# Gated-parallel decoder step: both transposes of a softmax block in one step, its values one step sooner

## The chip, the cores and the metric

One program on one core of one Trainium2 chip. The metric is device microseconds of one execution. The core has five engines with instruction queues of their own that run side by side and wait for each other through semaphores: TensorE (PE, with its weight loads listed as PEld), VectorE (DVE), ScalarE (ACT), GpSimd (POOL) and SyncE (SP), which here only issues transfers between the memory of the device and that of the core. Each engine works through its queue in order, so an instruction that waits holds up all that stand behind it on its engine.

## The reference

One decoder layer on 1024 prompt tokens and 64 sample tokens (8 sequences of 8), in float32:

```
u = rmsnorm(x); [a | q | k | v | g_a | g_b] = u @ w_in
branch A: multi-scale pooling of a, a linear map for each group, @ w_pa
branch B: 3 head groups of 4 heads, (window, dilation) = (128,1), (512,4), (2048,16):
    qb = query blocks of 128;  kb, vb = the block itself and the block before it
    s = qb . kb * 64**-0.5, masked;  p = exp(s - max) ;  den = sum(p);  o = p . vb / den
    the 3 groups' outputs are combined by weights proportional to their denominators, @ w_pb
h = x + (sigmoid(g_a) * A + sigmoid(g_b) * B) @ w_o
y = h + relu(rmsnorm(h) @ w_up)**2 @ w_down
```

The change touches the prompt's part of branch B alone: `p . vb` needs `p` with keys on the partitions, so the softmax is transposed before it is multiplied with the values.

## The kernel before, in words

Float32 matrices are split into two rounded parts, and each product of weights is made of three passes over these parts, so nearly all of the time is matmuls of 128x128 weights. The program runs in stages: the pooling input, then the queries, keys and values of group 2 (dilation 16), group 1 (dilation 4) and group 0 (dilation 1), then the gates, the two output branches, `w_o`, and the two halves of the feed-forward layer.

The attention is woven into the three middle stages. `qkv_part` makes one projection of one block of 128 tokens (`pqk` queries and keys together, `pq`, `pk` or `pv` one of them, each some 3 to 6 us of matmuls), and then calls `step()`; the wide ones (`pqk`) also call it in their middle. `step()` runs every pending piece of side work forward to its next `yield`: each is a Python generator, and what it issues between two yields stands on PE's queue between two pieces of projection. The order on PE is exactly the order in which the kernel issues (`manual_schedule`); on the other engines a scheduler sets it when the kernel is built, by its own estimate of times, so a move on PE also moves rows on DVE, ACT and the transfer queue.

For each block `b` of each group there is one generator: `attend` transposes the block's queries and keys (`tq`, line 673), and `attend_rest` goes on to `attention`, the function that changes. Its parts, by the lines of the profile:

- scores `sg` (line 690): matmuls of 64 rows, two heads side by side, into two PSUM tiles, one for each value of `e`
- softmax: for each of four heads a masked minimum on DVE (line 699, tile `sm`) and an exponential on ACT (line 700); the heads of `e` = 0 come first
- two yields, and then for each `e` the transposes `tp` (line 709) on PE, the copy of them to `pT` on ACT (line 712), and a yield
- values `po` (line 723): matmuls that fill 64 columns of the array, from both `pT`, and a copy to the tile `oc` on ACT (line 730, 733 or 736)

A block of group 0 after the first has two blocks of keys (`nk` = 2), as has every second block of group 1; the others have one, and half the transposes, scores and values. After `attention`, `attend_rest` stores `oc` (line 824) or, in group 0, starts `combine` (transposes `tw` of the weights, line 782, and spreading matmuls `sw`, line 791), and the store of its result (line 797). All transfers between the memories that the passage names go through SP's queue.

The buffers rotate: `short` gives PSUM tiles from four, `sm` and `pT` have two each.

Names: in the tables `tpg2b0` or `pog1b6` are the transposes of group 2, block 0 and the values of group 1, block 6; the profile leaves block numbers out (`tpg2b`). `L116` on ACT and `L117` on DVE split weights that have come in (`raw_qkv`), `L657` scales queries or keys by their norm, `L664` copies a block's values out of PSUM, `L602` copies a block's tokens into natural order (`natt`), `L511` belongs to the pooling.

Of the kernel before, what the change touches and what calls it, by code (L numbers as in the profile page):

```python
# [37 lines left out]
def decoder_step(ctx, tc, i, o):  # L38
# [10 lines left out]
    def rr(p, shape, dt, name, tag, bufs):  # L49

        n = turn[p, tag] = turn.get((p, tag), -1) + 1
        return p.tile(shape, dt, name=name, tag=f"{tag}.{n % bufs}", bufs=1)
# [183 lines left out]
    def short(name):  # L236

        spare[0] = (spare[0] + 1) % 4
        if spare[0] == 4:
            return acc_p.tile([P, 512], F32, name=name, tag="acc.3", bufs=1)  # L240
        return ps.tile([P, 512], F32, name=name, tag=f"t.{spare[0]}", bufs=1)

    def short4(name):
        return short(name).rearrange("p (a b) -> p a b", a=4)
# [346 lines left out]
    def res8(blk):  # L591
        return blk // 2 + 4 * (blk % 2)
# [85 lines left out]
    def attention(g, b, keys, qT, name):  # L678


        st = md[:, b, 0, :] if g == 0 else sta[g][:, res8(b), :]
        nk = len(keys)
        mask = m3 if g == 2 else (m1 if nk == 2 else m1[:, P:])
        W = nk * P
        sc = [short(f"s{name}_{e}").rearrange("p (a b) -> p a b", a=2) for e in range(2)]
        for hp in range(2):
            for j, (kT, _) in enumerate(keys):
                for e in range(2):
                    rows = slice(e * HD, (e + 1) * HD)
                    t_.matmul(sc[e][:, hp, j * P:(j + 1) * P], qT[rows, hp, :], kT[rows, 2 + hp, :], start=True, stop=True)  # L690
        done.add(name)
        sms = []
        for e in range(2):
            sm = rr(ap, [P, 2, 256], F32, name=f"sm{name}_{e}", tag="sm", bufs=2)
            sms.append(sm)
            for hp in range(2):
                h = 2 * hp + e

                v_.tensor_tensor_reduce(sm[:, hp, :W], sc[e][:, hp, :W], mask, -1.0, -NEG, ALU.add, ALU.min, st[:, h:h + 1])
                s_.activation(sm[:, hp, :W], sm[:, hp, :W], AF.Exp, bias=st[:, h:h + 1], scale=-1.0,  # L700
                              accum_out=st[:, 4 + h:5 + h])
        yield
        yield
        pTs = []
        for e in range(2):
            tp = short4(f"tp{name}_{e}")
            for hp in range(2):
                for j in range(nk):
                    t_.transpose(tp[:, hp * nk + j, :], sms[e][:, hp, j * P:(j + 1) * P], ident)  # L709
            pT = rr(ap, [P, 4, P], F32, name=f"pT{name}_{e}", tag="pT", bufs=2)  # L710
            pTs.append(pT)
            s_.copy(pT[:, :2 * nk, :], tp[:, :2 * nk, :])
            if g == 0 and b % 2 and e == 0:
                assert {(1, "max"), (2, "max")} <= done
                of_pair[b // 2] = weights(b // 2)
            yield
        po = short(f"po{name}")[:, :256].rearrange("p (j t) -> p j t", j=2)

        for hp in range(2):
            for j, (_, vr) in enumerate(keys):  # L720
                for e in range(2):
                    h = 2 * hp + e
                    t_.matmul(po[e * HD:(e + 1) * HD, hp, :], vr[:, h * HD:(h + 1) * HD], pTs[e][:, hp * nk + j, :],  # L723
                              start=(j == 0), stop=(j == nk - 1))
        if b % 2 == 0:
            assert g or b < 4 or ("c", b // 2 - 2) in done
            pair[g] = rr(ap, [P, 512], F32, name=f"oc{name}", tag="oc", bufs=2)
        if g == 2:
            dst = pair[g].rearrange("p (u j l s) -> p j u l s", u=4, j=2, s=2)
            s_.copy(dst[:, :, :, :, b % 2], po.rearrange("p j (u l) -> p j u l", u=4))  # L730
        elif g == 1:
            dst = pair[g].rearrange("p (u j l) -> p j u l", u=4, j=2)
            s_.copy(dst[:, :, b % 2 * 2:b % 2 * 2 + 2], po.rearrange("p j (u l) -> p j u l", u=2))
        else:
            dst = pair[g].rearrange("p (j q l) -> p j q l", j=2, q=4)
            s_.copy(dst[:, :, :, b % 2 * 32:(b % 2 + 1) * 32], po.rearrange("p j (l q) -> p j q l", q=4))
# [4 lines left out]
    def weights(u):  # L741


        nm, den = md[:, 2 * u:2 * u + 2, :, :4], md[:, 2 * u:2 * u + 2, :, 4:]
        mm = ap2.tile([P, 2, 4], F32, name=f"cm{u}", tag="cm2")
        e = ap2.tile([P, 2, 3, 4], F32, name=f"ce{u}", tag="ce2")
        w = ap2.tile([P, 2, 3, 4], F32, name=f"cw{u}", tag="cw2")
        hl = ap2.tile([P, 2, 2, 3, 4], F32R, name=f"hl{u}", tag="hl")
        over = lambda t: t.unsqueeze(2).to_broadcast([P, 2, 3, 4])
        behind_pe(v_.tensor_reduce(mm, nm.rearrange("p b g h -> p b h g"), axis=AX.X, op=ALU.min))  # L750
        v_.tensor_tensor(e, over(mm), nm, op=ALU.subtract)
        s_.activation(e, e, AF.Exp)
        v_.tensor_tensor(w, e, den, op=ALU.mult)
        v_.tensor_reduce(mm, w.rearrange("p b g h -> p b h g"), axis=AX.X, op=ALU.add)
        v_.reciprocal(mm, mm)
        v_.tensor_tensor(w, e, over(mm), op=ALU.mult)
        s_.copy(hl[:, :, 0], w)
        v_.tensor_tensor(hl[:, :, 1], w, hl[:, :, 0].bitcast(F32), op=ALU.subtract)
        return hl.rearrange("p b s g h -> p b (s g h)").bitcast(F32)
# [1478 lines left out]
```

## Time and profile before

| | |
|---|---|
| time, 3 runs | 1402.63 us median (1401.01 to 1406.38) |
| the profiled execution | 1407.21 us, of which the span of its records is 1405.4 us |
| busy in the span | PE 1394.7 us (99%), PEld 1344.4, DVE 958.3, ACT 753.7, POOL 255.3 |
| mean granted TensorE clock | 0.999 of full speed |
| attention woven into the projections | about 90 to 416 us of the span |

PE is busy for 99% of the span. Its busy time is a modelled one: a matmul is listed with its whole passage through the array, and matmuls that follow each other overlap, so a short wait or a change of shape is hidden in the busy time. The start times don't hide it: what a group of matmuls costs the queue is the time from its start to the start of the next group. In the rows of the timeline the first column is the start in us from the span's beginning, the second how long the group took, and a bracket at the end gives idle time of the engine before it and what ended it.

### The profile page before, as it was taken

The page shows a single profiled execution, that of the slowest core. Times are in us where ns is not written, and L with a number is a line of the kernel's source. Part 1 is how long each engine was busy: PE and PEld are TensorE (multiplying, and loading weights), DVE is VectorE, ACT ScalarE, POOL GpSimd, SP SyncE. Part 2 cuts the span into 40 slices and gives each one's busy share as a digit, 9 for nine tenths or more (in the row PEclk, how much of TensorE's full clock was granted, in tenths as well). Part 3 has the DMA queues.
Part 4 walks back from the last instruction along what each step waited for, and adds up shares of the span by engine and source line. Part 5 has one row for each costly group of instructions (what it writes and reads, how often), then busy time and mean ns, then how long its engine had stood idle before and what let it go on. Part 6 is the DMA issues. An engine that isn't in the chain of part 4 may idle for free.

```text
span 1405.4 us, 29330 instructions
## 1 busy us (share of the span) xinstructions
PE 1394.7 (99%) x11101; PEld 1344.4 (96%) x11101; DVE 958.3 (68%) x1714; ACT 753.7 (54%) x1778; POOL 255.3 (18%) x362
## 2 busy tenths in 40 slices
PE   9999999999999999999999999999999999999998
PEld 8988987887999999999999999999999999999998
DVE  7778744776776767876468678665665686664566
ACT  8556775787765323563336455454554544444443
POOL 0744355676500000000000000000000000000100
PEclk9999999999999999999999999999999999999999
DMA  6455876755477777975468668856758988787674
GB/s 215 132 178 169 252 234 211 223 137 141 123 255 228 247 233 239 314 237 176 133 200 285 227 221 275 267 195 213 251 191 270 332 275 261 230 245 231 206 257 169
DMA packets 180701, 311.96 MB, mean 222 GB/s; under 512 B 26824, under 2 KB 82574, under 8 KB 178511
## 3 DMA queue, kind: packets, MB, share of 16 engines
q1 hardware_dynamic: 174926, 258.04, 57.0%
q0 software_dynamic: 5632, 52.04, 11.5%
q8 instruction: 87, 1.43, 0.4%
q14 instruction: 56, 0.45, 0.1%
HBM read 239.94 MB, written 122.12 MB: 258 GB/s over the span
## 4 chain that ended last, share of the span: by engine, by line
PE 70%; DMA 2%; DVE 1%; ACT 0%; issue 0%; SPq 0%; DVEq 0%; ACTq 0%
PE pz L1318 23%; PE pd L2096 23%; PE pg L1318 11%; PE ph L200 7%; PE pab L1318 4%; DMA raw_ab<-in_w_ab_dram 1%; DMA raw_d<-in_w_down_dram 0%; ACT places L116 0%; PE pog0b L723 0%; PE sg0b L690 0%; PE tpg0b L709 0%; PE pk L200 0%; PE pv L200 0%; SPq L127 0%; DVE places L117 0%
## 5 line engine op out<-in xcount | busy, mean ns | idle before, releaser
L2096 PE MATMUL pd<-places 128*128 128x272 f32 x2688 | 332.0, 287 | 0.7 <-DVE t L1960 0.7
L2096 PEld LDWEIGHTS pd<-places 128*128 128x128 f32 x2688 | 331.6, 188 | 0.9 <-DVE t L1960 0.9
L116 ACT ACTIVATE places<-raw_d 128x544 fp32r<-128x544 f32 (+1 forms) x176 | 110.5, 646 | 161.9 <-DMA raw_d<-z_d 51.3
L2136 POOL DMA_DIRECT2D out_kv_sample_dram<-in_cache_kv_dram x96 | 47.0, 490 | 793.1 <-ACT places L116 583.9
L117 DVE TENSOR_TENSOR places<-raw_d,places 128x544 fp32r<-128x544 f32 (+1 forms) x176 | 122.5, 711 | 91.7 <-ACT places L116 90.7
L1318 PE MATMUL pz<-act,places 128*128 128x280 f32 (+1 forms) x1080 | 139.4, 287 | 0.0
L1318 PEld LDWEIGHTS pz<-act,places 128*128 128x128 f32 x1080 | 135.9, 188 | 0.0
L200 PE MATMUL ph<-act,places 128*128 128x280 f32 (+1 forms) x768 | 96.6, 287 | 0.0
L200 PEld LDWEIGHTS ph<-act,places 128*128 128x128 f32 x768 | 96.0, 188 | 0.1
L1318 PE MATMUL pg<-act,places 128*128 128x264 f32 (+1 forms) x576 | 75.6, 288 | 0.0
L1318 PEld LDWEIGHTS pg<-act,places 128*128 128x128 f32 x576 | 72.6, 188 | 0.6 <-issue 0.3
L1318 PE MATMUL pz<-places,apart 128*128 128x264 f32 (+1 forms) x528 | 67.9, 287 | 0.0
L1318 PEld LDWEIGHTS pz<-places,apart 128*128 128x128 f32 x528 | 66.6, 188 | 0.0
L200 PE MATMUL pqk<-places,act 128*128 128x512 f32 x240 | 62.2, 410 | 0.0
L1318 PE MATMUL pz<-act,apart 128*128 128x264 f32 (+1 forms) x456 | 59.1, 287 | 0.0
L1318 PEld LDWEIGHTS pz<-act,apart 128*128 128x128 f32 x456 | 57.5, 188 | 0.1
L200 PEld LDWEIGHTS pqk<-places,act 128*128 128x128 f32 x240 | 45.8, 196 | 10.1
L874 POOL TENSOR_TENSOR pck<-pck,qs 128x256 f32<-128x256 f32 x64 | 49.9, 812 | 21.6 <-DMA pck<-own_d 7.6
L652 POOL TENSOR_TENSOR mr<-ms,mhalf 128x4 f32<-128x4 f32 (+2 forms) x39 | 51.3, 1317 | 2.9 <-POOL ms L651 0.2
L329 PE MATMUL a<-act,places 128*128 128x384 f32 (+1 forms) x288 | 50.9, 334 | 1.0 <-ACT act L307 0.9
L1318 PE MATMUL pab<-ab,places 128*128 128x264 f32 (+1 forms) x384 | 50.6, 287 | 0.2 <-DVE gg L1643 0.2
L329 PEld LDWEIGHTS a<-act,places 128*128 128x128 f32 x288 | 47.9, 188 | 2.9 <-ACT act L307 1.8
(436 smaller groups left out, 2811.7 us busy)
## 6 DMA issues: line engine op xcount, KB each, us to landing
out_kv_sample_dram<-in_cache_kv_dram POOLq DMA_DIRECT2D x72, 480.0 KB, 4.8
raw_d<-z_d SPq DMA_DIRECT2D x112, 272.0 KB, 4.3
z_d<-t SPq DMA_DIRECT2D x80, 272.0 KB, 4.0
raw_d<-in_w_down_dram SPq DMA_DIRECT2D x80, 256.0 KB, 3.8
raw_u<-in_w_up_dram SPq DMA_DIRECT2D x64, 256.0 KB, 4.0
raw_qkv<-in_w_in_dram SPq DMA_DIRECT2D x36, 256.0 KB, 3.8
own_d<-in_cache_kv_dram POOLq DMA_DIRECT2D x32, 256.0 KB, 3.4
pck<-own_d SPq DMA_DIRECT2D x16, 512.0 KB, 4.7
```

Source lines behind the costliest of these rows:

```text
L116: ins = s_.activation(dst_hi, src, AF.Copy)
L117: v_.tensor_tensor(dst_lo, src, dst_hi.bitcast(F32), op=ALU.subtract)
L200: last_mm[0] = t_.matmul(out, lhs(a, k), rhs(b, k), start=(j == 0), stop=(j == len(terms) - 1))
L329: last_mm[0] = t_.matmul(pts[m][:, :n], wt[:, a, kk, m * P:(m + 1) * P], act4[b][kk][:, :, part4(c)], start=(p == 0 and kk == 0), stop=(p ...
L652: last_norm[0] = g_.tensor_tensor(r[:n, :H], ms[:n, :H], mhalf[:n, :H], op=ALU.pow)
L874: ins = g_.tensor_tensor(out, *others, op=ALU.mult)
L1318: last_mm[0] = t_.matmul(out[c], lhs(*term), rhs(*term, c), start=(first and n == 0), stop=(n == len(terms) - 1), skip_group_check=not first)
L2096: last_mm[0] = t_.matmul(outs(chain[t], Q)[c], A[:, a, t * P:(t + 1) * P], Z[:, b, c], start=(fresh and f == 0 and n == 0), stop=(f == NG ...
L2136: ins = g_.dma_start(d, a)
```

## The change

The last `yield` of the loop over `e` goes out of the loop. Before, one step held the transposes of `e` = 0, the next step those of `e` = 1, and the one after that the values. Now one step holds both transposes, and the next one the values. All that follows in the block's generator comes a step sooner as well: the copy to `oc`, the stores, and in group 0 `combine`.

```
@@ -713,7 +713,7 @@
             if g == 0 and b % 2 and e == 0:
                 assert {(1, "max"), (2, "max")} <= done
                 of_pair[b // 2] = weights(b // 2)
-            yield
+        yield
         po = short(f"po{name}")[:, :256].rearrange("p (j t) -> p j t", j=2)
 
         for hp in range(2):
```

The number of matmuls stays the same. Three places in the built programs show what moves. The first is PE's queue at the first block of group 2, with `act` and `places` the split tokens and weights, `cst` the identity. Before:

```order
L709 MATMUL tpg2b0_0_1253<-cst_58,smg2b0_0_1153 128x128 x2
L200 MATMUL pqk2_3_1264<-places_77,act0_71 128x512 x12
L709 MATMUL tpg2b0_1_1288<-cst_58,smg2b0_1_1158 128x128 x2
L690 MATMUL sg2b1_0_1293<-qkTg2b1_1194 128x128
L690 MATMUL sg2b1_1_1294<-qkTg2b1_1194 128x128
L690 MATMUL sg2b1_0_1293<-qkTg2b1_1194 128x128
L690 MATMUL sg2b1_1_1294<-qkTg2b1_1194 128x128
L200 MATMUL pqk2_3_1264<-places_77,act0_71 128x512 x4
L200 MATMUL pqk2_3_1264<-places_77,act1_72 128x512 x8
L723 MATMUL pog2b0_1339<-pTg2b0_0_1256,v2_0_767 64x128
L723 MATMUL pog2b0_1339<-pTg2b0_1_1291,v2_0_767 64x128
```

And with the change:

```order
L709 MATMUL tpg2b0_0_1253<-cst_58,smg2b0_0_1153 128x128 x2
L709 MATMUL tpg2b0_1_1258<-cst_58,smg2b0_1_1158 128x128 x2
L200 MATMUL pqk2_3_1269<-places_77,act0_71 128x512 x12
L723 MATMUL pog2b0_1293<-pTg2b0_0_1256,v2_0_767 64x128
L723 MATMUL pog2b0_1293<-pTg2b0_1_1261,v2_0_767 64x128
L723 MATMUL pog2b0_1293<-pTg2b0_0_1256,v2_0_767 64x128
L723 MATMUL pog2b0_1293<-pTg2b0_1_1261,v2_0_767 64x128
L690 MATMUL sg2b1_0_1300<-qkTg2b1_1194 128x128
L690 MATMUL sg2b1_1_1301<-qkTg2b1_1194 128x128
L690 MATMUL sg2b1_0_1300<-qkTg2b1_1194 128x128
L690 MATMUL sg2b1_1_1301<-qkTg2b1_1194 128x128
L200 MATMUL pqk2_3_1269<-places_77,act0_71 128x512 x4
```

The values of block 0 have moved ahead of the scores of block 1, and half a projection now lies between the transposes and the values where a whole one and a bit lay between the first transposes and them. Counted over the whole queue, values stand directly ahead of scores 12 times (2 before), transposes `tp` directly ahead of scores 2 times (14 before), values directly ahead of transposes `tq` 2 times (13 before), and there are 24 groups of `tp` in place of 48. Behind the attention the queues of PE, DVE, ACT and POOL hold the same rows in the same order.

The second place is ACT's queue at block 5 of group 2, where weights for group 1 come in. Before:

```order
L116 ACTIVATE places_77<-raw_qkv1_2_0_1957 128x512
L664 ACTIVATE v2_7_1723<-pv2_7_2047,stats_64 128x256
L511 ACTIVATE am3_1845<-pl3_2_2083,cols_59 128x4x80
L712 COPY pTg2b5_0_2090<-tpg2b5_0_2087 128x256
L116 ACTIVATE places_77<-raw_qkv1_2_512_2012 128x512
L116 ACTIVATE places_77<-raw_qkv1_2_1024_2028 128x512
L712 COPY pTg2b5_1_2156<-tpg2b5_1_2153 128x256
```

With the change:

```order
L116 ACTIVATE places_77<-raw_qkv1_2_0_1962 128x512
L664 ACTIVATE v2_7_1728<-pv2_7_2047,stats_64 128x256
L511 ACTIVATE am3_1851<-pl3_2_2083,cols_59 128x4x80
L116 ACTIVATE places_77<-raw_qkv1_2_512_2019 128x512
L712 COPY pTg2b5_0_2090<-tpg2b5_0_2087 128x256
L712 COPY pTg2b5_1_2095<-tpg2b5_1_2092 128x256
L116 ACTIVATE places_77<-raw_qkv1_2_1024_2035 128x512
L730 COPY ocg2b4_1986<-pog2b5_2158 128x2x4x32
```

Both copies of `pT` now stand behind one split of weights that stood behind the first of them, and the copy of the values follows.

The third place is ACT's queue at block 6 of group 1. Before:

```order
L664 ACTIVATE v0_0_3682<-pv0_0_3898,stats_64 128x256
L712 COPY pTg1b6_0_3944<-tpg1b6_0_3941 128x256
L657 ACTIVATE qk0_0_3681<-pk0_0_3854,mr0_0_1_3880 128x64 x4
L700 ACTIVATE smg1b7_0_3956,sta1_712<-smg1b7_0_3956,sta1_712 128x256 x2
L712 COPY pTg1b6_1_3999<-tpg1b6_1_3996 128x256
L700 ACTIVATE smg1b7_1_3961,sta1_712<-smg1b7_1_3961,sta1_712 128x256 x2
```

With the change:

```order
L664 ACTIVATE v0_0_3689<-pv0_0_3898,stats_64 128x256
L657 ACTIVATE qk0_0_3688<-pk0_0_3854,mr0_0_1_3880 128x64 x4
L712 COPY pTg1b6_0_3944<-tpg1b6_0_3941 128x256
L712 COPY pTg1b6_1_3949<-tpg1b6_1_3946 128x256
L700 ACTIVATE smg1b7_0_3961,sta1_712<-smg1b7_0_3961,sta1_712 128x256 x2
L700 ACTIVATE smg1b7_1_3966,sta1_712<-smg1b7_1_3966,sta1_712 128x256 x2
```

Here the copies of `pT` have moved behind the four scalings of keys, and the second copy ahead of the exponentials of block 7.

2 lines of the change are left out of this document (1 added, 1 removed).

## The prediction

> **What bounds the kernel now.** I read the page first, then PE's waits, the windows around the longest of them, and the timeline of PE and ACT at the blocks. The first two rows are of the page, the third of PE's waits (engine and tile, what it waited for, us in total, times, longest).
>
> ```profile
> span 1405.4 us, 29330 instructions
> PE 1394.7 (99%) x11101; PEld 1344.4 (96%) x11101; DVE 958.3 (68%) x1714; ACT 753.7 (54%) x1778; POOL 255.3 (18%) x362
> PE sg2b L690 <- DVE qkTg2b L676: 2.3, 1, 2.3
> ```
>
> PE is the bound of the whole program, and its longest wait is 2.3 us. So a change in the attention counts by two things alone: what a group of matmuls costs PE's queue, and how long PE waits for DVE or ACT. What the other engines do in the meantime is free until PE waits for it. Behind the attention the queues are the same, so a shift of PE there is carried to the end.
>
> The long wait has a second price. Two stretches of 3.41 us each, the wait and what follows it (length, then busy time and instructions of PE, PEld, DVE, ACT, POOL, then the granted clock):
>
> ```profile
> 101.96:105.37 3.41, 1.14 (x12) 0.78 (x11) 3.41 (x9) 1.20 (x5) 0.00 (x0) 1.00 0.73 298
> 105.37:108.78 3.41, 3.41 (x9) 2.63 (x10) 3.41 (x10) 0.23 (x1) 0.00 (x0) 0.50 0.35 125
> ```
>
> After a stretch with 1.14 us of work, PE has half its clock for 3.41 us: 1.7 us of work are lost on top of the wait of 2.27. [...]
>
> **The change part by part.** *Costs on PE's queue.* Block 4 of group 0 shows the order before: transposes for `e` = 0, half a projection, transposes for `e` = 1, scores, half a projection, values (of the block before), `tq`, projection.
>
> ```profile
> 355.41 0.60 PE L709 MATMUL tpg0b<-cst,smg0b 128*128 128x128 f32 x4
> 355.76 3.13 PE L200 MATMUL pq<-places,natt 128*128 128x256 f32 x24
> 358.97 0.60 PE L709 MATMUL tpg0b<-cst,smg0b 128*128 128x128 f32 x4
> 359.50 0.49 PE L690 MATMUL sg0b<-qkTg0b,qkTg0b 64*128 64x128 f32 x4
> 360.59 3.11 PE L200 MATMUL pk<-places,natt 128*128 128x256 f32 x24
> 364.11 1.09 PE L723 MATMUL pog0b<-pTg0b,v 128*64 128x128 f32 x16
> 365.13 0.66 PE L673 MATMUL tqg0b<-cst,qk 128*128 128x128 f32 x4
> 365.55 3.06 PE L200 MATMUL pv<-places,natt 128*128 128x256 f32 x24
> ```
>
> By starts, four transposes cost 0.35 us ahead of a projection and 0.53 ahead of scores (0.18 more: the array goes from all rows to 64). Scores cost 1.09, values 1.02, `tq` behind values 0.42. What the new order puts together stands elsewhere in the trace: values ahead of scores, and `tq` not behind values.
>
> ```profile
> 208.80 0.66 PE L723 MATMUL pog1b<-pTg1b,v 128*64 128x128 f32 x8
> 209.39 0.49 PE L690 MATMUL sg1b<-qkTg1b,qkTg1b 64*128 64x128 f32 x4
> 210.48 3.07 PE L200 MATMUL pqk<-places,act 128*128 128x512 f32 x12
> 312.97 0.60 PE L673 MATMUL tqg0b<-cst,qk 128*128 128x128 f32 x4
> 313.32 3.08 PE L200 MATMUL pv<-places,natt 128*128 128x256 f32 x24
> ```
>
> Scores behind values cost the same 1.09, and the half as many values ahead of them 0.59, against half of 1.02, so that neighbourhood costs 0.08 at most, and I take nothing; `tq` elsewhere costs 0.35, 0.07 less. Joined transposes lose something: four of them directly ahead of others cost 0.43 (274.74 to 275.17, quoted below), so eight cost 0.43 + 0.35 = 0.78 in place of 2 x 0.35, 0.08 more. The lead from a projection into the values is there in both orders and cancels. By the counts of the order: 14 - 2 = 12 transitions from transposes to scores go, 12 x 0.18 = 2.2 us; 13 - 2 = 11 `tq` get cheaper, 11 x 0.07 = 0.8; 24 joins cost 24 x 0.08 = 1.9. **Sum: -1.1 us.** Bounds: nothing at all, or -2.5 if joining were free.
>
> *Waits.* The values now stand where the second transposes stood, and need both copies to `pT`, which ACT can make only half a projection after the transposes. I took for every one of the 24 blocks the end of the first copy, added one copy more (0.40 us for 128x256, 0.60 for 128x512), and held it against the start of the second transposes plus their own time. Eighteen fit. One more, block 0 of group 0, would lack its last exponentials if PE came as early as now, but by the sum below PE is later there. Five places decide.
>
> Block 0 of group 2 (PE, then ACT):
>
> ```profile
> 101.89 0.38 PE L709 MATMUL tpg2b<-cst,smg2b 128*128 128x128 f32 x2
> 104.55 0.72 PE L690 MATMUL sg2b<-qkTg2b 64*128 64x128 f32 x8 [2.27 <-DVE qkTg2b L676]
> 102.26 0.43 ACT L712 COPY pTg2b<-tpg2b 128x256 f32<-128x256 f32 x1
> 102.71 0.46 ACT L712 COPY pTg2b<-tpg2b 128x256 f32<-128x256 f32 x1
> ```
>
> Both copies are done by 103.17, the values take 0.59 and end at 103.8, and the scores behind them wait for DVE until 104.55 as they do now. So the values run inside a wait that is there anyway: **-0.6 us**. The idle time of that stretch falls from 2.27 to about 1.7. Whether this spares the half clock (-1.7) no row says: the lost 0.8 at 279.32 (below) didn't bring it, 2.27 did, and 1.7 is nearer to the latter. I take 0 and keep -1.7 as the bound.
>
> Block 5 of group 2:
>
> ```profile
> 165.51 0.38 PE L709 MATMUL tpg2b<-cst,smg2b 128*128 128x128 f32 x2
> 165.67 0.37 ACT L712 COPY pTg2b<-tpg2b 128x256 f32<-128x256 f32 x1
> 166.35 0.63 ACT L116 ACTIVATE places<-raw_qkv 128x512 fp32r<-128x512 f32 x1 [0.31 <-DMA raw_qkv<-in_w_in_dram]
> 167.99 0.35 ACT L712 COPY pTg2b<-tpg2b 128x256 f32<-128x256 f32 x1
> ```
>
> PE comes to the values at 165.7. The copies stand behind the split of 166.35, which waits for its weights: 166.98 + 0.37 + 0.25 = 167.6, a wait of 1.9. If the weights come earlier (ACT frees their buffer sooner in the new order), it is ACT's own queue, 165.67 + 0.7 = 166.4, a wait of 0.7. Behind the waiting values stand `tq` and the next projection. I take the middle: **+1.3**.
>
> Block 5 of group 1:
>
> ```profile
> 274.74 0.60 PE L709 MATMUL tpg1b<-cst,smg1b 128*128 128x128 f32 x4
> 275.17 0.60 PE L673 MATMUL tqg1b<-cst,qk 128*128 128x128 f32 x4
> 279.32 1.09 PE L723 MATMUL pog1b<-pTg1b,v 128*64 128x128 f32 x14 [0.38 <-ACT pTg1b L712]
> 275.08 0.61 ACT L712 COPY pTg1b<-tpg1b 128x512 f32<-128x512 f32 x1
> ```
>
> The copies now stand together and end near 276.2, PE comes at 275.17: a wait of 1.05, but the wait ahead of 279.32, 0.8 with the lost starts, goes. **+0.25**, within 0 and +1.
>
> Blocks 6 and 7 of group 1:
>
> ```profile
> 292.53 0.38 PE L709 MATMUL tpg1b<-cst,smg1b 128*128 128x128 f32 x2
> 296.21 0.66 PE L709 MATMUL tpg1b<-cst,smg1b 128*128 128x128 f32 x4
> 298.02 2.37 PE L200 MATMUL pqk<-places,natt 128*128 128x512 f32 x9
> 293.13 0.38 ACT L712 COPY pTg1b<-tpg1b 128x256 f32<-128x256 f32 x1
> 293.38 0.94 ACT L657 ACTIVATE qk<-pk,mr 128x64 f32<-128x64 f32 x4
> 297.12 0.49 ACT L700 ACTIVATE smg1b<-smg1b,sta 128x256 f32<-128x256 f32 x1
> ```
>
> PE comes to the values of block 6 at 292.75. The copies, behind the scalings, run from 293.9 to 294.6: a wait of 1.85. Then values, half a projection (2.9) and eight transposes, from 298.15; these need the exponentials, done at 297.6, and don't wait again. The projection of 298.02 comes at 299.9, of which 0.44 are transposes that had been paid later: **+1.45**, within +0.8 (if the scalings are early) and +1.9.
>
> Block 5 of group 0:
>
> ```profile
> 384.18 0.60 PE L709 MATMUL tpg0b<-cst,smg0b 128*128 128x128 f32 x4
> 384.49 0.60 ACT L712 COPY pTg0b<-tpg0b 128x512 f32<-128x512 f32 x1
> 385.33 0.63 ACT L712 COPY pTg0b<-tpg0b 128x512 f32<-128x512 f32 x1
> ```
>
> PE comes at 384.6, the second copy ends near 385.65: 1.0, of which some 0.3 replaces hesitation that the scores behind show already. **+0.7**, within 0 and +1.
>
> *Transfers.* The store of `oc`, and with it `st`, `md`, the loads for `combine` and its stores, come one to five places sooner in SP's queue, past loads of weights (`raw_qkv`) and of caches.
>
> ```profile
> L824 SPq EVENT_SEMAPHORE  x8: 17/704/4106, 123.1 to 310.5; - x8
> ```
>
> SP waits a median of 0.7 us, once 4.1, for these stores already; their data is a step sooner too, so I cost this at nothing. If that cover goes, a load of weights is late by up to 4 us, and ACT's split and then PE with it: it is in the upper bound of block 5, group 2.
>
> The sum is -1.1 - 0.6 + 1.3 + 0.25 + 1.45 + 0.7 = **+2.0 us**. On the profiled execution's 1407.2 (span 1405.4) it gives 1409.2; that execution lies 4.6 above the median of the three runs, so I forecast 1402.6 + 2.0 = **1404.6**.
>
> **The rivals.** *The waits don't come* (ACT's order moves enough that the copies are there in time) and the half clock behind 101.96 goes: -1.1 - 0.6 - 1.7 = -3.4, **1399.2**. For it speaks that 18 blocks have room and that all five waits are under 2 us; against it that at three of them the new order of ACT itself puts work ahead of the copies. [...]
>
> *The half clock comes again.* The waits of block 5, group 2 (up to 1.9) and block 6, group 1 (1.85) fall into one stretch of 3.41 us each. If 1.14 us of work in a stretch is not the limit but 1.5 is, each costs 1.7 more: 2.0 + 3.4 = +5.4, **1408.0**, slower than before. [...]
>
> *It doesn't do what it says.* At half the blocks values still don't stand beside scores, and savings and waits cancel: **1402.6**.
>
> **How the numbers follow.** The forecast has 0.55, no waits 0.18, half clock again 0.17, nothing 0.10. The range goes from the first rival to just past the second, **1399 to 1408.5**. A measurement of this kernel can tell about 0.5% (7.0 us) from no change: faster than 1395.6 is reached by no case, slower than 1409.6 only by the second rival with the upper bounds of all waits (+1.9, +1, +1.9, +1). Faster 0.05, same 0.87, slower 0.08.
>
> **What would show it.** Right, if in the changed profile values start within 0.6 us of the scores' start at short blocks and scores behind them cost 1.09; if `tp` groups of eight cost near 0.78; if PE's waits name `pTg2b`, `pTg1b` and `pTg0b` on ACT, at blocks 5 and 6; and if scores of group 2, block 1 still start near 104.5. Wrong, if joined transposes cost 0.7 or 1.0; if a wait for `pT` exceeds 2 us or a stretch other than that at 105 has a clock under 1; or if the time leaves 1399 to 1408.5 for a place outside 90 to 416 us.

## The result

The changed kernel takes 1410.2 us (median of eight, 1408.2 to 1414.4), the kernel before 1403.6 on the same chip: 1.0053 of it, with a 95% interval of 1.0042 to 1.0063. On a second chip it was 1.0072 (1.0053 to 1.0091). The change makes the kernel slower by 7 to 10 us. The forecast was +2.0, its range ended at 1408.5.

The first rows of the page of the changed kernel, whose profiled execution took 1409.2 us:

```profile
span 1407.4 us, 29341 instructions
PE 1393.2 (99%) x11101; PEld 1344.6 (96%) x11101; DVE 953.2 (68%) x1714; ACT 753.1 (54%) x1778; POOL 255.6 (18%) x362
```

PE is busy for 1.5 us less than before (1393.2 against 1394.7) and idle for 14.2 instead of 10.7, the rest of each span. From the list of PE's waits (what waited, for what; us in total, times, longest), in this profile:

```profile
PE pog2b L723 <- ACT pTg2b L712: 2.0, 2, 1.7
PE sft L1114 <- DVE sres L1109: 1.6, 1, 1.6
PE pog1b L723 <- ACT pTg1b L712: 1.5, 3, 0.7
...
PE pog0b L723 <- ACT pTg0b L712: 0.8, 1, 0.8
PE tpg0b L709 <- ACT smg0b L700: 0.7, 1, 0.7
```

and in a second profile of the changed kernel (span 1410.6):

```profile
PE pz L1318 <- ACT t_e L1883: 2.2, 1, 2.2
PE sft L1114 <- DVE sres L1109: 1.6, 1, 1.6
PE pog1b L723 <- ACT pTg1b L712: 1.4, 2, 0.7
...
PE pog0b L723 <- ACT pTg0b L712: 0.7, 1, 0.7
...
PE pog2b L723 <- ACT pTg2b L712: 0.6, 2, 0.4
```

The values (`po`) now wait for the copies to `pT`, 4.3 us in one profile and 2.7 in the other, and the waits at `sft` (1.6) and at the last transposes (0.7) are new and repeat exactly. The wait of 2.3 at the scores of group 2, the longest before, is gone. What it was is the first question, since by the two profiles alone the change costs 2.0 us (1407.4 against 1405.4) and by the medians 6.6.

### The profile page after: what moved, and what is told of

It is laid out like the page before. It is cut to its first block, busy times and chain, and to the rows that moved or that the text cites. A ratio compares the mean times of both kernels' runs of the same rounds, so it can differ in the third digit from the quotient of the medians.

```text
span 1407.4 us, 29341 instructions
## 1 busy us (share of the span) xinstructions
PE 1393.2 (99%) x11101; PEld 1344.6 (96%) x11101; DVE 953.2 (68%) x1714; ACT 753.1 (54%) x1778; POOL 255.6 (18%) x362
## 4 chain that ended last, share of the span: by engine, by line
PE 91%; DMA 3%; ACT 2%; DVE 2%; issue 1%; POOL 1%; SPq 0%; DVEq 0%; ACTq 0%; POOLq 0%
PE pz L1318 24%; PE pd L2096 24%; PE pg L1318 11%; PE ph L200 7%; PE pab L1318 5%; PE pqk L200 4%; PE pv L200 4%; PE a L329 4%; PE pq L200 1%; PE pk L200 1%; DMA raw_qkv<-in_w_in_dram 1%; ACT qk L657 0%; DMA attn_d<-ocg0b 0%; PE sg1b L690 0%; DMA out_kv_prompt_dram<-kw 0%
```

## The experiments

All ratios are to the kernel before, run in turn with each kernel on the same chip; they lie within 0.0003 of the ratios of the means, while the times beside them are medians. A stretch of 3.41 us at half clock lowers the mean clock of an execution by 3.41 x 0.5 / 1405 = 0.0012, and part of another one falls into the end of some executions (the last 1.64 us of the span in the first profile of the changed kernel, at 0.50); so a mean of 1.000 has none inside, 0.998 or less at least one. Of 109 executions of the kernel before in this study 11 had 0.998 or less, of the 12 of the changed kernel 7.

### One group at a time

The change for one group g of the three, here 2:

```diff
-            yield
+            if e or g != 2: yield
```

> The change made for the eight blocks of group 2 alone; groups 1 and 0 keep the yield inside the loop. Theory A (the cost is waits of PE for the copies to pT; the size is what the two profiled executions show between the starts of the same matmuls): the scores of the first block of group 1 come 1.6 us sooner in the changed kernel than before, so this part alone gives 1403.6 - 1.6 = 1402.0, with no stretch at half clock near 105 us and a wait for pTg2b of 1.5 to 2 us near 151 us. Theory B (what separates the two kernels is how often a stretch of 3.41 us at half clock falls into an execution, since 5 of 8 executions of the changed kernel have a mean clock of 0.998, one stretch more than 0.999): this part with its wait of 1.7 us brings such stretches, 1404.5 to 1406, with a mean clock of 0.998 in half of the executions or more.

> The change made for the blocks of group 1 alone. Theory A: between the scores of the first block of group 1 and those of the first of group 0 the changed kernel loses 1.9 us against before (from -1.6 to +0.3), so 1403.6 + 1.9 = 1405.5, with waits for pTg1b of 0.4 to 0.8 us at blocks 4, 5 and 6 and for the exponentials at block 5. Theory B: 1.9 more than that for executions at a mean clock of 0.998, a median near 1406.5.

> The change made for the blocks of group 0 alone. Theory A: from the first scores of group 0 to the end of the attention the changed kernel loses 2.4 us against before, so 1403.6 + 2.4 = 1406.0, with waits near 333 us for pTg0b (0.9) and near 401 to 409 us. Theory B: the same within 1 us, since the waits there are short; more than half of the executions at 0.999. In both the three parts add up to the whole, +6.6, only if they don't act on each other: A's sum is +2.7.

Measured: group 2 alone 1403.7, ratio 1.0012 (1.0003 to 1.0022); group 1 alone 1408.2, 1.0041 (1.0027 to 1.0055); group 0 alone 1407.8, 1.0037 (1.0024 to 1.0049). Each part alone is slower, group 2 too, for which theory A had a gain; neither theory had any of the three. The parts add up to 0.9%, more than the 0.53 of the whole, so they seem to act on each other; against the 0.72 of the second chip that isn't clear of the noise. A had its numbers from the two first profiles, and the profile of group 0 alone shows what was wrong in them. Up to group 0 its program is the one before, yet the scores of block 2 of group 2 start at 114.81 us there and at 118.97 in the profile before. DVE's addition at line 525, ahead of the copy to `qkT` that these scores need, in the kernel before:

```profile
100.26 1.36 DVE L525 TENSOR_TENSOR ts<-act,act 128x544 f32<-128x544 f32 x2 [3.39 <-DMA ts_d<-ts]
```

and in the kernel with group 0 alone changed:

```profile
96.70 1.36 DVE L525 TENSOR_TENSOR ts<-act,act 128x544 f32<-128x544 f32 x2 [1.08 <-DMA ts_d<-ts]
```

The same instructions, with a transfer that landed 3.6 us sooner. The 4.16 us between the two profiles are a matter of the execution: 1407.2 - 4.2 = 1403.0 is where the medians of the runs before lie (1402.5 to 1403.6).

### The kernel before once more

> The kernel before once more, for a second profile. Theory C (the wait of 2.27 us at 104.55 and the half clock behind it were an accident of the one execution that was profiled: there DVE's addition at line 525 waited 3.4 us for a transfer to ts_d to land, in the profile of the part of group 0 it waited 1.1, with the same instructions up to that point): the scores of block 1 of group 2 start 3.5 to 4.2 us sooner than 104.55, at 100.4 to 101, no stretch at half clock near 105, span near 1400.7. Rival (the wait belongs to the program): the scores at 104.5 and the half clock again, span 1405.

Its span was 1405.0, and PE's longest wait was there again:

```profile
PE sg2b L690 <- DVE qkTg2b L676: 2.2, 1, 2.2
```

So theory C's numbers missed, and the rival's came: the second profile had the wait too and, by its mean clock of 0.998, a stretch at half clock. But this execution took 1406.7 where the 25 runs beside it have a median of 1402.75. Among the 16 profiles of this study in which DVE makes that copy, PE's wait there (at the scores, or at the values now ahead of them) is 2.1 us or more in five, 1.1 to 1.3 in two, and at most 0.4 in nine. It is chance, not rare, and two profiles of one kernel happened to have it. That it isn't the program shows where kernels have one order of instructions up to this place: group 1 alone and group 0 alone have that of the kernel before, without the wait; group 2 alone has that of the changed kernel, with a wait of 2.3 that neither profile of the changed kernel has.

### Joining without moving the values

A second yield behind the joined transposes:

```diff
-            yield
+        yield; yield
```

> Both transposes in one step, as in the change, but a second yield behind them, so that the values stay where they were before. Theory A (values that come before their copies are the cost): no wait for pT but that of before; joining gives 12 x 0.18 less at scores and costs 24 x 0.08, -0.3 us, and waits for exponentials that are due a step sooner give 0.5 to 1.5: 1404 to 1405. Rival (joining is the cost, because the second exponentials are due a step sooner and PE waits for them): 1407 or more, with waits for smg1b and smg0b of over 3 us in all.

Measured 1405.2, ratio 1.0019 (1.0007 to 1.0031): no wait for `pT` is left in the profile, and of the change's 0.53 to 0.72% the larger part is gone. So the values' early place costs 0.3 to 0.5%, the joining 0.2. The joining was expected to give 1404 to 1405, but not by what its profile shows. PE's longest wait, then POOL and ACT ahead of it:

```profile
PE tps L1001 <- ACT p L995: 4.3, 1, 4.3
```

```profile
297.68 5.70 POOL L874 TENSOR_TENSOR pcv<-pcv,sc 128x256 f32<-128x256 f32 x8 [4.71 <-DMA pcv<-in_cache_kv_dram]
304.30 1.85 POOL L651 TENSOR_TENSOR ms<-ms,stats 128x8 f32<-128x8 f32 x1 [0.92 <-DVE ms L645]
306.23 2.08 POOL L652 TENSOR_TENSOR mr<-ms,mhalf 128x8 f32<-128x8 f32 x1
...
308.34 1.75 ACT L657 ACTIVATE qk<-pqk,mr 128x64 f32<-128x64 f32 x8 [7.80 <-POOL mr L652]
```

POOL in the kernel before at the same place:

```profile
300.36 2.33 POOL L874 TENSOR_TENSOR pcv<-pcv,sc 128x256 f32<-128x256 f32 x4 [3.08 <-DMA pcv<-in_cache_kv_dram]
...
306.24 0.35 POOL L651 TENSOR_TENSOR ms<-ms,stats 128x8 f32<-128x8 f32 x1
306.66 1.66 POOL L652 TENSOR_TENSOR mr<-ms,mhalf 128x8 f32<-128x8 f32 x1
```

PE is 4.8 us earlier in this execution than in that one (301.05 against 305.89 at the first scores of group 0), and POOL's norm factors (lines 651 and 652) come at the same time, 308.3. Of the 4.8 the chance wait of that profile is 4.2. Group 0 alone has the order of the kernel before up to there, and its execution lacks the wait: the scores start at 302.19, the factors are done at 304.11. Against that the factors are 4.2 us late here, in three parts: POOL ends its work on `pcv` at 303.38 instead of 302.07, then waits 0.92 for DVE, then takes 4.0 for the two lines instead of 2.1.

In SP's order the third load of `pcv` has gone behind the load of `osm`, ahead of which SP issues nothing for 1.6 us (290.79 to 292.42; in the changed kernel's list 1.1 us of waiting at this load is for the stores to `so_d`); it stands there in every kernel here that joins the transposes of all of group 1 in the earlier step. This fits the first part, and by way of DVE perhaps the second. It doesn't explain the third: of the eight profiles with the load moved, the two lines take 4.0 to 4.6 us in three (this one, and below the kernels with group 1's stores and with all stores put back), and these alone have a wait at `tps` (4.3, 1.5 and 2.0). In the other five, the two of the changed kernel among them, they take 2.0 to 2.1 as before, and PE doesn't wait there. What makes them slow is open. The test is to leave group 1 out:

```diff
-            yield
+            for _ in range(1 if g == 1 else 2 * e): yield
```

> Transposes joined in the earlier step and values where they were, as in the run of that kind before, but for groups 2 and 0 alone; group 1 is as before, and SP's loads of pcv stand where they stood. Theory I (the 2.7 us of the joining come from group 1: there the second load of pcv is moved behind the stores to so_d and the load of osm, POOL gets to the norm factors 4.2 us late, and PE waits 4.3 us at tps with two stretches at half clock, in a part of the executions): 1402.0 to 1403.0, no execution with a mean clock under 0.998. Rival H (joining disturbs ACT and DVE at all blocks): 1404.5 or more.

Measured 1403.2, ratio 0.9999 (0.9989 to 1.0009), and no execution under 0.998. The norm factors are done 2.9 us after the first scores of group 0 start (307.42 and 304.57), where it was 7.3 with group 1 joined (308.31 and 301.05) and 2.4 before (308.32 and 305.89). As theory I had it, joining in groups 2 and 0 costs nothing that can be seen, and the 0.2% come with group 1. That the moved load is their cause isn't shown: the run leaves out all of group 1, and in five profiles the load has moved without the wait.

Joining in the later of the two steps, where nothing is due sooner:

```diff
-        yield
+        yield; yield
         yield
         pTs = []
...
-            yield
+        yield
```

> Both transposes in one step, but in the later of the two steps, so that neither the exponentials nor the copies are due sooner than before, and the values and stores stay where they were. Theory A (joining costs the queue 24 x 0.08 = 1.9 us less 2 x 0.18; all else in the cost of the joined transposes in the earlier step, 2.7, is that something is due sooner): 1403.8 to 1404.5, with no wait for smg1b or smg0b. Rival H (joining disturbs ACT and DVE, since both copies come together and the buffer sm is freed a step later): 1405.5 or more.

Measured 1410.7, 1.0050 (1.0033 to 1.0067). The rival was right: PE's waits are now for DVE (1.8 at the values of group 1, 1.3 at `qkT`, where the wait comes by chance, 0.7 at `oc`) and the busy time of PE rises to 1396.7. The later step is no free place to join in.

### Group 0: the copy that waits for a buffer

The last 20 us of the attention in the changed kernel, ACT and then DVE:

```profile
399.02 0.37 ACT L736 COPY ocg0b<-pog0b 128x256 f32<-128x256 f32 x1 [4.04 <-DMA attn_d<-ocg0b]
399.29 0.22 ACT L1102 ACTIVATE sfe<-sfe 128x12 f32<-128x12 f32 x1
```

```profile
399.54 0.18 DVE L1103 TENSOR_TENSOR sfw<-sfe,osm 128x12 f32<-128x12 f32 x1 [3.78 <-ACT sfe L1102]
...
399.84 0.41 DVE L699 CUSTOM_DVE_ANT_0 smg0b<-sg0b,cst 128x256 f32<-128x256 f32 x1
```

and ACT in the kernel before:

```profile
395.52 0.21 ACT L1102 ACTIVATE sfe<-sfe 128x12 f32<-128x12 f32 x1 [0.53 <-DVE sfe L1101]
...
398.83 0.37 ACT L736 COPY ocg0b<-pog0b 128x256 f32<-128x256 f32 x1
```

Before, the values of block 6 were copied into `oc` at 398.83, behind the small exponential of line 1102. Now their copy is due at 395. It needs one of two buffers `oc`; that one holds blocks 2 and 3 until its store to `attn_d` (issued at 392.81) has landed. ACT stands for 4.0 us (4.3 in the second profile), the exponential behind it, DVE behind that, and the maxima of block 7 start at 399.84 where they started at 396.07. PE waits for them at the transposes (0.7) and at `sft` (1.6). Two edits test it. First, one more yield ahead of these values in the changed kernel:

```diff
-        yield
+        for _ in range(1 + ((g, b) == (0, 6))): yield
```

> The change with one more yield ahead of the values of block 6 of group 0 alone, so that these stand where they stood before. Theory D (ACT's copy of these values into oc, line 736, comes too early: one of the two buffers oc is still held by the combination of blocks 2 and 3 and its store to attn_d, ACT waits 4.0 us, and behind it stand the exponential of line 1102, DVE's line 1103, the maxima of block 7, its transposes and sft): the wait of ACT for attn_d is gone, the maxima of block 7 start 3 us sooner, PE's waits for sft (1.6) and smg0b (0.7) go, 1410.2 - 2.4 = 1407.8, and down to 1406.2 where a stretch at half clock went with them. Rival (the end of the attention has slack and gives the time back): 1409.5 or more.

Measured 1408.2, 1.0035 (1.0022 to 1.0047), against 1.0053: some 2 us better, as expected, though ACT still waits:

```profile
399.25 0.37 ACT L736 COPY ocg0b<-pog0b 128x256 f32<-128x256 f32 x1 [1.91 <-DMA attn_d<-ocg0b]
```

but by now the exponential and the maxima (394.47) stand ahead of it. PE's wait at the last transposes is gone, the one at `sft` is 1.1 instead of 1.6. The intervals meet, so this run alone is no proof. The second edit is clearer on the size: group 0 alone, without its blocks 6 and 1 (at block 1 the copies to `pT` stand behind ACT's casts for the next projection):

```diff
-            yield
+            if e or g or b in (1, 6): yield
```

> The change for group 0 alone, without its blocks 1 and 6, which are as before. Theory D (the 5.2 us of group 0 sit at these two places: 1.7 at the values of block 1, behind ACT's casts for the next projection, 3.5 with its half clock from the copy to oc of block 6): 1402.5 to 1403.5. Rival F (undone at one block, the cost comes up at another, as in the run with six blocks undone): 1405 or more.

Measured 1404.4, 1.0011 (1.0003 to 1.0020), where all of group 0 cost 1.0037, with mean clocks of 1.000 in nine of eleven executions, where all five of group 0 had 0.998. So some 70% of group 0's cost sits at these two blocks, by ratios from two chips; the time lies between theory D's (up to 1403.5) and rival F's (1405 or more), and what block 6 costs by itself this run doesn't tell. A third buffer for `oc` would test the cause directly; it wasn't run.

### Group 1: a store ahead of loads

With group 1 alone changed, PE's waits include

```profile
PE pog1b L723 <- ACT pTg1b L712: 2.3, 3, 1.2
PE pog0b L723 <- ACT pTg0b L712: 1.9, 1, 1.9
```

The second is in group 0, whose code is unchanged. SP's queue in that kernel, ahead of it:

```profile
304.47 0.56 SPq L824 DMA_DIRECT2D o_d<-ocg1b  x1
...
306.39 0.42 SPq L945 DMA_DIRECT2D kt<-in_kT_dram  x1
308.31 0.34 SPq L776 DMA_DIRECT2D ow<-o_d  x1
308.76 4.40 SPq L850 DMA_DIRECT2D pcv<-in_cache_kv_dram  x4
```

and before:

```profile
309.17 1.27 SPq L850 DMA_DIRECT2D pcv<-in_cache_kv_dram  x2
310.54 0.56 SPq L824 DMA_DIRECT2D o_d<-ocg1b  x1
...
315.04 0.55 SPq L776 DMA_DIRECT2D ow<-o_d  x1
```

The load of `ow` reads what the store wrote, SP issues nothing ahead of it for 1.5 us (306.81 to 308.31), and loads of `pcv` that were ahead of it are now behind. The edit, made on top of the change for group 1 alone, puts the stores of group 1 back by one step:

```diff
         oc = pair[g]
-        yield
+        for _ in range(1 + (g == 1)): yield
```

> The change for group 1 alone, with one more yield ahead of the stores of oc and of the statistics, so that these stand in SP's queue where they stood before. Theory E (the stores are due a step sooner, and SP waits at the load of ow for the store to land, 1.5 us, ahead of loads of pcv; POOL's weighting of pcv is late by that, and with it the norm factors at line 652, ACT's scalings at line 657, the second copy to pT behind them, and PE at the values of block 0 of group 0, 1.9 us, with a stretch at half clock behind it): that wait and the half clock are gone, 1408.2 - 2 to - 3.7: 1404.5 to 1406.2. Rival (the waits for pT inside group 1, 2.3 us, are the whole cost, and the wait in block 0 of group 0 was chance): 1407.5 or more.

Measured 1405.9, 1.0018 (1.0006 to 1.0030), against 1.0041 (1.0027 to 1.0055): as theory E had it, and the wait in group 0 is gone, though the wait of 1.5 at `tps` has come. In the changed kernel SP stands at `ow` ahead of loads of `pcv` in the same way (308.41 to 310.00 in its first profile, 1.5 us of it listed as a wait for the store to `o_d`), yet the values of that block don't wait in either profile: this wait is one of group 1 alone.

### Repairs that didn't hold

The changed kernel with all stores put back, and block 6 of group 0 as above:

```diff
-        yield
+        for _ in range(1 + ((g, b) == (0, 6))): yield
...
         oc = pair[g]
-        yield
+        for _ in range(2): yield
```

> The change with all stores of oc and of the statistics, the loads for the combination and the combination itself one step later than in the change (where they stood before), and the values of block 6 of group 0 one step later. Theory E + D (a large part of the cost comes from these, not from the values beside the scores): 2.3 us from the stores as measured in group 1 alone and 2 from block 6: 1410.2 - 4.3 = 1406, ratio 1.0025. Rival G (the cost is the waits for the copies to pT themselves, in all groups, 4.3 us in the profile of the change, which stay): 1408.5 or more.

Measured 1411.0, 1.0052 (1.0032 to 1.0072): nothing gained, rival G. The waits for `pT` are 4.3 us in its profile, and PE waits 2.0 at `tps` as with the joined transposes. The change for 18 blocks, without the six that showed a wait:

```diff
-            yield
+            if e or (g, b) in ((2, 4), (1, 4), (1, 5), (1, 6), (0, 1), (0, 6)): yield
```

> The change for 18 of the 24 blocks; the six at which profiles show a wait for the copies, the exponentials or the buffer oc (block 4 of group 2, blocks 4, 5 and 6 of group 1, blocks 1 and 6 of group 0) keep the yield inside the loop. Theory A (the cost sits in these blocks): the waits are gone and the queue's gain is left, 18 x 0.17 = 3 us at most: 1399.5 to 1401.5. Rival F (the cost sits in the shifted order of loads and stores and of ACT's work at all blocks, and comes up elsewhere): 1404 or more, with waits at blocks that had none.

Measured 1409.0, 1.0035 (1.0021 to 1.0049): rival F. Its profile has 1.6 us of waits for `pT` at a block of group 1 that was put back and 1.1 at one of group 2 that hadn't waited. The changed kernel with the second copy to `pT` on DVE:

```diff
-            s_.copy(pT[:, :2 * nk, :], tp[:, :2 * nk, :])
+            (v_.tensor_copy if e and g < 2 else s_.copy)(pT[:, :2 * nk, :], tp[:, :2 * nk, :])
```

> The change, with the second of a block's two copies to pT on DVE in place of ACT, in groups 1 and 0; the queues of PE, SP and POOL are those of the change, row for row. Theory A (the values wait for ACT's queue: the second copy stands behind the first and behind what ACT has ahead of it): the waits for pT of groups 1 and 0, 2.3 us in one profile of the change and 2.1 in the other, fall below 1.2, and the time to 1.0040 of before or less. Rival J (the first copy is as late as the second, since both stand behind the same work of ACT, so a free second copy helps nothing, and DVE's own work is later): waits as before the edit, 1.0053 or more.

(In SP's order one store, `smp_d`, came two rows later; the rest is as in the change.) Measured 1414.7, 1.0080 (1.0064 to 1.0096): rival J. PE's waits:

```profile
PE sft L1114 <- DVE sres L1109: 2.6, 1, 2.6
PE pog1b L723 <- ACT pTg1b L712: 2.5, 3, 1.1
```

The values still wait for the first copy, on ACT, and the end of the attention waits a microsecond longer for DVE. One value waits 0.7 for its second copy, on DVE. So the copies are late for what stands ahead of both more than for each other.

The changed kernel itself beside these:

> The changed kernel once more, beside the two below on one chip, and for a second profile. Expected: 1.0053 of the time before, near 1410. What its profile repeats belongs to the program: PE's waits for pT at block 4 of group 2 (1.8), blocks 4 and 5 of group 1 (0.5 and 0.8) and block 1 of group 0 (0.9), ACT's wait of 4.0 for attn_d ahead of line 736, PE's wait of 1.6 at sft; what it doesn't repeat within half of that is chance.

1413.2, 1.0072 (1.0053 to 1.0091). Of the listed waits `sft` and group 1's block 5 repeat in size and group 0's block 1 nearly; that at block 4 of group 2 was 1.7 in one profile and 0.4 in the other. The wait of 2.2 at line 1318, behind the attention where the four engines' queues are the same, is in this profile alone. From its last spreading matmuls (415.83) to the end it takes 994.8 us, where the first profile takes 989.8 and the two of the kernel before 989.7 and 989.0: some 5 us of this execution are lost behind the attention, and whether the change brings them is open.

### A faster kernel?

Two waits of the kernel before taken away: the values of block 5 of group 1 a step later, the copy to `qkT` of block 1 of group 2 on ACT:

```diff
-        (v_.tensor_copy if g == 2 else s_.copy)(dst[:, 2:, :n], tp[:, 2:, :n])
+        (v_.tensor_copy if g == 2 and name != "g2b1" else s_.copy)(dst[:, 2:, :n], tp[:, 2:, :n])
...
-            yield
+            for _ in range(1 + (e and (g, b) == (1, 5))): yield
```

> The kernel before with two of its waits taken away: the values of block 5 of group 1 one step later (they wait 0.8 to 1.3 for pT in every profile in which group 1 is as before), and the copy to qkT of block 1 of group 2 on ACT in place of DVE, so that the scores at 104.55 no longer stand behind DVE's wait for ts_d. Theory C (that wait is chance and costs 4 us with its half clock in a part of the executions): -1.0 for the first and -4 in a fifth of the executions for the second: a median near 1401.5, and no executions above 1405. Rival (the scores then wait for ACT instead, or the time is lost behind): 1402.5 or more with the same spread.

Measured 1404.5, 1.0015 (0.9996 to 1.0033), with a spread of 1401.0 to 1414.3: no gain, as the rival had it. The copy on ACT together with the joined transposes of groups 2 and 0:

```diff
-        (v_.tensor_copy if g == 2 else s_.copy)(dst[:, 2:, :n], tp[:, 2:, :n])
+        (v_.tensor_copy if g == 2 and name != "g2b1" else s_.copy)(dst[:, 2:, :n], tp[:, 2:, :n])
...
-            yield
+            for _ in range(1 if g == 1 else 2 * e): yield
```

> Transposes joined in the earlier step in groups 2 and 0 alone, as in the run before, and the copy to qkT of block 1 of group 2 on ACT in place of DVE; PE's order is the same. Theory C (the wait for DVE comes in a part of the executions, 2.1 us and with a stretch at half clock 3.8): the wait is gone from the profile, the scores of that block start near 102.0, and the time is 0.9975 to 0.999 of before. Rival (DVE's or ACT's shifted order gives it back at another place): 1.000 or more, with a wait elsewhere of as much.

Measured 1402.9, 0.9993 (0.9979 to 1.0007). The wait is gone from the profile, as theory C had it, and eleven of twelve executions have a mean clock of 1.000 (six of eleven without that edit), but the time can't be told from before. No kernel tried here beats the one before beyond its interval.

## Why the prediction was wrong

**The queue's costs** were right where the rows show them. In the changed kernel's timeline:

```profile
334.35 1.57 PE L723 MATMUL pog0b<-pTg0b,v 128*64 128x128 f32 x16 [0.85 <-ACT pTg0b L712]
335.85 0.49 PE L690 MATMUL sg0b<-qkTg0b,qkTg0b 64*128 64x128 f32 x4
...
336.94 1.43 PE L200 MATMUL pqk<-places,natt 128*128 128x512 f32 x5
...
357.17 1.04 PE L709 MATMUL tpg0b<-cst,smg0b 128*128 128x128 f32 x8
357.96 3.05 PE L200 MATMUL pq<-places,natt 128*128 128x256 f32 x24
```

Eight joined transposes cost 357.96 - 357.17 = 0.79 (forecast 0.78), scores behind values 336.94 - 335.85 = 1.09 (forecast 1.09). The sum of -1.1 no run shows: the joining in groups 2 and 0 came to 0.9999, within 1.4 us of nothing either way. The bound of -2.5 for free joining was added up wrongly: 12 x 0.18 + 11 x 0.07 is 2.9.

**The term of block 0, group 2 (-0.6)** failed in its base. I took the wait of 2.27 us as part of the program because the queue showed a releaser, DVE's copy. DVE in turn was behind a transfer, and that one's landing changes from one execution to the next (3.6 us between the two shown). In nine of sixteen profiles there is next to no wait to hide the values in; in the two of the changed kernel those of block 0 waited 0.3 and 0.2 for `pT` themselves. The same mistake stood in the sum's base: I saw that the profiled execution was 4.6 above the median and set it aside, without asking which wait made it so. With 4.2 us taken off, the two profiled executions differ by 6.2 (1409.2 - 1403.0), and the medians by 6.6.

**The waits for `pT`** had the right size and half the wrong places. Forecast were 5.2 us at five places (1.3, 1.05, 1.85, 1.0, and none in block 0), of which some replaced old waits. Measured are 4.3 and 2.7 as listed. A listed wait isn't all that it costs: the sixteen values of 334.35 took 1.50 us to the start of the scores, where the next block's, without a wait, took 1.02 (348.67 to 349.69), and eight took 0.86 instead of 0.59. Over the listed waits this adds 2.0 and 1.8, so 6.3 and 4.5 in all. Block 5 of group 2, forecast at 1.3, doesn't wait: its weights came in time. Block 4 does:

```profile
151.73 0.63 ACT L116 ACTIVATE places<-raw_qkv 128x512 fp32r<-128x512 f32 x1 [2.68 <-DMA raw_qkv<-in_w_in_dram]
152.26 0.30 ACT L657 ACTIVATE qk<-pq,mr 128x64 f32<-128x64 f32 x1
152.46 0.64 ACT L712 COPY pTg2b<-tpg2b 128x256 f32<-128x256 f32 x2
```

It is the mechanism I described, a split that waits for weights ahead of the copies, one block sooner. Block 6 of group 1 waits 0.4 in one profile instead of 1.85, block 5 of group 0 not at all, and blocks 4 of group 1 and 1 of group 0, which I had among the eighteen that fit, do wait (0.4 to 0.6 and 0.7 to 0.85). Slack that is read from one execution of the old order doesn't tell which block of the new order is short, since ACT's order moves too. Only the total came out, and with half the places wrong that is luck.

**"Transfers: at nothing"** is the step that failed outright. I looked at the stores that move, and at SP's wait for their data. In the changed kernel the cost is the buffer that a store holds: by moving the values I moved the copy into `oc`, and never asked when its buffer comes free. In both profiles PE waits 2.3 us for what stands behind that copy (0.7 and 1.6), and with block 6 a step later 1.0053 becomes 1.0035. In kernels that make a part of the change two more showed: a store that a later load waits for (group 1 alone, 1.0041 to 1.0018 when put back), and a load of `pcv` that changed sides with other rows (in the joining, its share of the 0.2% not shown). Each of them stops an engine that works in order, and what is queued behind has nothing to do with the values.

By an estimate from these rows, the forecast of 2.0 without the 0.6 of block 0, with 2.3 for the buffer and with 1.7 for a half clock in seven of twelve executions (1.0 in the mean) comes to 5.9, of 6.6 measured.

**The rival of the half clock** came nearest, 1408.0, but by another place and with its limit set too low. I set it at 1.5 us of work in a stretch, and expected it at blocks 5 and 6. In group 0 alone, at the wait for `sft`, the half clock came behind 1.80 (first the stretch with the wait, then the next; columns as in the prediction):

```profile
403.39:406.80 3.41, 1.80 (x15) 1.60 (x14) 3.41 (x10) 2.93 (x7) 0.00 (x0) 1.00 0.37 127
406.80:410.21 3.41, 3.41 (x17) 3.41 (x16) 2.49 (x4) 0.94 (x2) 0.00 (x0) 0.50 0.94 281
```

In the changed kernel's first profile the same wait left a little more work in its stretch, 1.98, and the next one (409.05 to 412.47) had its full clock, 1.00:

```profile
405.64:409.05 3.41, 1.98 (x18) 1.59 (x12) 3.41 (x11) 1.98 (x6) 0.00 (x0) 1.00 0.23 66
```

By the mean clocks seven of twelve executions of the changed kernel have a stretch at half clock, and two of ten with block 6 a step later. Neither profile of the changed kernel has one inside, so that these 1.7 us are part of its typical time is inferred from the mean clocks, not seen.

**What stays open.** The three groups' costs, 1.7, 5.8 and 5.2 us, make 12.7 where the whole has 6.6 to 10.6; why they cover each other in part I can't say in full. One piece is shown: the wait at block 0 of group 0, 1.9 in group 1 alone, isn't there in the changed kernel. Which of the waits for `pT` cost how much no run shows, since putting them back one block at a time brought others. Nor do I know why the repairs that help alone (block 6, the stores of group 1) give nothing together.

## What to carry to other kernels

Before a long wait is counted, follow it back: if it ends at a transfer, check the profiled time against the median, and look at several more executions; here the second one had the wait too. When instructions are moved in a tightly ordered kernel, their own cost is the least of it: list every wait that moves with them, the buffer they write, the store that frees it, the loads that change places in the queue, and for each the engine that stops and what is queued behind it. And expect the reserves that one profile shows at 18 of 24 places to be gone in the new order: repairing the places that show a wait brings out the next.

## What the runs showed of the hardware

The half clock came behind stretches in which PE still worked. Two of them, from group 1 alone and from the joined transposes; the stretch behind the first has 0.50 (322.21 to 325.62), and so have the two behind the second (309.78 to 316.61):

```profile
318.80:322.21 3.41, 1.47 (x20) 1.15 (x20) 0.98 (x3) 2.81 (x12) 2.33 (x4) 1.00 0.68 176
```

```profile
306.37:309.78 3.41, 1.30 (x6) 0.72 (x4) 1.91 (x12) 1.44 (x8) 3.33 (x4) 1.00 0.74 226
```

and one behind which it didn't come, from the kernel with group 1's stores put back, whose profiled execution has a mean clock of 1.000:

```profile
309.70:313.11 3.41, 1.88 (x9) 1.22 (x7) 0.14 (x1) 3.35 (x17) 2.23 (x5) 1.00 0.80 217
```

In these profiles 1.14 us of work (the kernel before), 1.30, 1.47 and 1.80 (group 0 alone) had 0.50 behind them, and 1.72 (the changed kernel, 149.64 to 153.05, with 1.00 to 156.47), 1.88 and 1.98 didn't. The borders of stretches that no record shows are counted from one that it does, in steps of 3.4133 us, an estimate: the kernel before has halved stretches from 105.37 and, behind its last instruction, from 1405.85, which are 381 such steps apart. So in group 0 alone 1.6 us of idle time in one stretch (3.41 - 1.80) cost 1.7 more (0.5 x 3.41), and in the changed kernel 1.7 (3.41 - 1.72) cost nothing more. Nor did a wait of 2.1 at the scores of group 2 that lay across the border of two, in the kernel with the transposes joined in groups 2 and 0:

```profile
99.81:103.22 3.41, 2.02 (x9) 1.36 (x7) 3.41 (x6) 2.89 (x12) 1.21 (x3) 1.00 0.56 179
103.22:106.64 3.42, 2.71 (x17) 2.30 (x18) 3.42 (x10) 0.00 (x0) 0.00 (x0) 1.00 0.33 137
```

The stretch behind them (106.64 to 110.05) has 1.00 too, where the wait of 2.27 in the kernel before, inside one stretch, had 0.50 behind it: of two waits of nearly one length, the one that fell into a single stretch brought the half clock.

Second, the time in which a small store lands. The one to `attn_d` was issued at 392.81, and ACT went on at 399.02, 6.2 us later; in the kernel with block 6 a step later 7.6 passed (391.62 to 399.25), while the median of the four such stores in the kernel before is 3.6. Why it is so slow at this place I haven't tried.
